# Mean squares by one block product instead of column sums and transposing spreads

## The chip, the cores and the metric

The kernel runs on one core of one Trainium2 chip. The metric is the device time of a launch in microseconds (us); of two kernels the one with the smaller time is better. A core has TensorE (PE in the profile, its weight loads PEld), VectorE (DVE), ScalarE (ACT), GpSimd (POOL) and SyncE (SP), and DMA queues that SP, ACT and POOL issue to.

## The reference

A trunk of two layers over x of 512 positions by 1024 channels, all in float32. Each layer has two sub-layers:

```python
h = rms_norm(x, norm1_g[l])
proj = h @ w_in[l]
za, xb, q, k, v, g = jnp.split(proj, splits, axis=-1)
ya = spatial_gating(jax.nn.gelu(za), a_vnorm_g[l], a_ws[l], a_bs[l])
yb = multiscale_pool(xb, b_w[l], b_scale[l])
yc = retention(q, k, v, g, c_norm_g[l])
x = x + jnp.concatenate([ya, yb, yc], axis=-1) @ w_out[l]
x = x + conv_ffn(rms_norm(x, norm2_g[l]), w_up[l], conv_w[l], conv_b[l], w_down[l])
```

`rms_norm` divides a position's 1024 channels by the root of their mean square plus EPS = 1e-6. `retention` ends with a norm per head: eight heads of 64 channels, each with its mean taken off and divided by the root of its mean square plus EPS, then a gain, then a product with silu(g). A last `rms_norm` follows the second layer.

## The kernel before

Channels lie on partitions and the 512 positions on the free dimension: x is eight tiles X[k] of 128 channels by 512 positions. Weights come as slots of 1024 columns through SP's queue; each is split into a rounded part `hi` (ScalarE) and the rest `lo` (VectorE), and a product in near-float32 precision is three fast matmuls (`mm3`, lines 310 to 312: hi by hi, hi by lo, lo by hi). A few products run in plain fp32; the profile shows each of those as two records.

`mixing` computes the first sub-layer as a list of short steps, `MIX`, in program order. Q, K, G, B and U are projections of one slot, A one of two; s and y are the scores and the output of one head; v centres the values; B and m are pooling and its map; a is the spatial gating; r and c are the head norm. The framework orders each engine's instructions when the kernel is built, by this order, by planned costs and by which buffers are free, so the steps may overlap. At the end `oproj` forms each output tile from eight operands `cat`, in the order in which `MIX` finishes them, the first six of tiles 0 and 1 ahead of the last two.

Head norm. After two heads (a pair p) `ymix` leaves their output in a tile `y_sb` and its square in `ysq`. Step r, `yvar`, sums the squares of each head for 128 positions at a time: the square is the stationary operand and a table of two columns, `selt`, the moving one, so that the sums lie with positions on partitions (eight columns a pair). `rsqrt` computes the reciprocal square root on these small tiles, with a term from the table `epst`, by ScalarE's Sqrt, VectorE's reciprocal and one refinement step. Step c, `ycat`, spreads the result back to channels: for each head and each 128 positions, one column, broadcast, is the stationary operand and the identity the moving one. Then it multiplies `y_sb` by gain and factor, by the gate, and splits the product for `oproj`.

Second norm. `feed` collects the squares of X in one tile `s`. `stats` (line 291) sums it over channels in the same way into four columns and calls `rsqrt`; `spread` (line 298) brings the factor back to all 128 partitions and ScalarE copies it to `bc`. In `ffn` the first two up projections run ahead of the factor: `stats` follows the first, `spread` the second. Their results are multiplied by `bc` (line 725).

Other tiles of 512 columns come from one pool, `U`, of `UBUFS` = 58 buffers; PSUM has eight banks of one tile each.

Of the kernel before, what the change touches and what calls it, by code (L numbers as in the profile page):

```python
# [10 lines left out]
F32 = mybir.dt.float32  # L11
F32R = mybir.dt.float32r
AF = mybir.ActivationFunctionType
ALU = mybir.AluOpType
AX = mybir.AxisListType

P = 128
D = 1024
T = 512
DEPTH = 2  # L20
KT = D // P
NT = T // P
AW = 256
CW = 512
HEADS = 8
DH = 64
# [4 lines left out]
EPS = 1e-6  # L31

C_N1, C_N2, C_VG, C_BS, C_CG, C_CW, C_CB = 0, 8, 16, 18, 20, 24, 24 + 3 * 2 * FT
# [4 lines left out]
GROUPS = (8, 8, 6)  # L38
SLOTS_PER_LAYER = 98
WBUFS = {"raw": 5, "hi": 5, "lo": 5}  # L40
UBUFS = 58
LOOK = 3
FIN = 3
WARM = 9
MIX = (
    "Q0 K0 v23 G0 v01 Q1 s0 K1 G1 s1 y0 Q2 s2 y1 K2 s3 B0 y2 Q3 s4 y3 K3 "
    "m0 r01 s5 y4 A s6 G2 y5 G3 s7 y6 y7 r2 c1 c0 B1 r3 a U1 c2 c3 m1 U0"
).split()
WIDE = {"A": 2}
SLOT = {}  # L50
# [139 lines left out]
def trunk(ctx: ExitStack, tc: tile.TileContext, xT, wflat, vec, ws_t, bias_t, bw, rope, dmask, vdec, geps, cnt, sel, out):  # L190
    nc = tc.nc
    cp = ctx.enter_context(tc.tile_pool(name="const", bufs=1))
# [10 lines left out]
    def PS(name):  # L203
        return psp.tile([P, T], F32, tag="ps", name=name)
# [15 lines left out]
    make_identity(nc, ident)  # L220
    ones = cp.tile([P, 1], F32, name="ones")
    nc.vector.memset(ones, 1.0)
    eps = cp.tile([P, 1], F32, name="eps")
    nc.vector.memset(eps, EPS)
    selt = cp.tile([P, 2], F32, name="selt")
# [5 lines left out]
    nc.gpsimd.dma_start(out=dmt, in_=dmask)  # L231
    dect = cp.tile([P, NT, HEADS], F32, name="dect")
    nc.gpsimd.dma_start(out=dect, in_=vdec)
    epst = cp.tile([P, 4, NT, 2], F32, name="epst")
    nc.gpsimd.dma_start(out=epst, in_=geps)

    zero = U("zero", F32R)
    nc.vector.memset(f(zero), 0.0)
# [1 line left out]
    for i in range(WARM):  # L240
        nc.tensor.matmul(busy, zero[:, :P], zero, start=True, stop=True)

    def rsqrt(src, n, scale, name, eps_t=None):
        m = sp.tile([P, n], F32, tag="rm", name=name + "m")
        r0 = sp.tile([P, n], F32, tag="r0", name=name + "a")
        if eps_t is None:
            nc.vector.tensor_scalar(
                out=m, in0=src, scalar1=-0.5 * scale, scalar2=-0.5 * EPS, op0=ALU.mult, op1=ALU.add
            )
            nc.scalar.activation(out=r0, in_=src, func=AF.Sqrt, scale=scale, bias=eps)  # L250
        else:
            nc.vector.scalar_tensor_tensor(
                out=m, in0=src, scalar=-0.5 * scale, in1=eps_t, op0=ALU.mult, op1=ALU.subtract
            )
            nc.scalar.activation(out=r0, in_=m, func=AF.Sqrt, scale=-2.0)
        nc.vector.reciprocal(r0, r0)
        nc.vector.tensor_tensor(out=m, in0=m, in1=r0, op=ALU.mult)
        nc.vector.tensor_tensor(out=m, in0=m, in1=r0, op=ALU.mult)
        r = sp.tile([P, n], F32, tag="rr", name=name + "r")
        nc.vector.scalar_tensor_tensor(out=r, in0=m, scalar=1.5, in1=r0, op0=ALU.add, op1=ALU.mult)  # L260
        return r

    class Norm:
        def __init__(self, name, col):
# [4 lines left out]
        def feed(self, k):  # L269
            n = f"{self.name}_{k}"  # L270
            g = vecs[:, self.col + k : self.col + k + 1]
            hi = U(n + "h", F32R)
            lo = U(n + "l", F32R)
            nc.scalar.activation(out=hi, in_=X[k], func=AF.Identity, scale=g)
            nc.vector.scalar_tensor_tensor(out=lo, in0=X[k], scalar=g, in1=f(hi), op0=ALU.mult, op1=ALU.subtract)
            self.h.append(hi)
            self.l.append(lo)
            sq = U(n + "q")
            nc.scalar.activation(out=sq, in_=X[k], func=AF.Square)
            if k == 0:  # L280
                self.s = sq
                warm = sp.tile([P, 1], F32, tag="warm", name=n + "w")
                nc.scalar.activation(out=warm, in_=sq[:, :1], func=AF.Sqrt)
            else:
                nc.vector.tensor_tensor(out=self.s, in0=self.s, in1=sq, op=ALU.add)

# [7 lines left out]
        def spread(self):  # L294
            n = self.name
            rb = PS(n + "rb")
            for b in range(NT):
                nc.tensor.matmul(
                    rb[:, b * P : (b + 1) * P],
                    self.tok[:, b : b + 1].to_broadcast([P, P]),  # L300
                    ident,
                    start=True,
                    stop=True,
                )
            self.bc = U(n + "bc")
            nc.scalar.copy(self.bc, rb)

    def mm3(ps, wt, k, xh, xl, first, last, more=False):
        hi, lo = wt
# [34 lines left out]
    def mixing(l, nm, nxt):  # L344
# [4 lines left out]
        def col(c):  # L349
            return vecs[:, vc + c : vc + c + 1]  # L350
# [97 lines left out]
        y_sb = {}  # L448
        yn = {}
# [48 lines left out]
        yr = {}  # L498

        def yvar(ps):  # L500
            n = 2 * NT
            vps = PS(f"yv{l}_{ps[0]}")
            for i, p in enumerate(ps):
                sq = ysq.pop(p)
                for b in range(NT):
                    o = i * n + 2 * b
                    nc.tensor.matmul(vps[:, o : o + 2], sq[:, b * P : (b + 1) * P], selt, start=True, stop=True)
            m = n * len(ps)
            et = epst[:, ps[0] : ps[-1] + 1].rearrange("p a b o -> p (a b o)")
            r = rsqrt(vps[:, :m], m, 1.0 / DH, f"yr{l}_{ps[0]}", et)  # L510
            for i, p in enumerate(ps):
                yr[p] = r[:, i * n : (i + 1) * n]

        def ycat(p):
            r = yr.pop(p)
            rb = PS(f"yb{l}_{p}")
            for b in range(NT):
                for o in range(2):
                    nc.tensor.matmul(
                        rb[o * DH : o * DH + DH, b * P : (b + 1) * P],  # L520
                        r[:, 2 * b + o : 2 * b + o + 1].to_broadcast([P, DH]),
                        ident,
                        start=True,
                        stop=True,
                    )
            y = y_sb.pop(p)
            nc.vector.scalar_tensor_tensor(out=y, in0=y, scalar=col(C_CG + p), in1=rb, op0=ALU.mult, op1=ALU.mult)
            g = yn.pop(p)
            nc.vector.tensor_tensor(out=g, in0=g, in1=y, op=ALU.mult)
            cat[4 + p] = split(g, f"c{l}_{4 + p}")  # L530

# [175 lines left out]
    def ffn(l, nm, nxt):  # L707
# [4 lines left out]
        def up(j, s):  # L712
            c2 = []
            for which in range(2):
                n = f"{l}_{j}_{which}"
                ps = proj("up" + n, s + which, hs, ls)
                if j == 0:
                    (nm.spread if which else nm.stats)()
                c2.append(ps)
            for which, ps in enumerate(c2):  # L720
                n = f"{l}_{j}_{which}"
                t = which * FT + j
                w = [vecs[:, vc + C_CW + i * 2 * FT + t : vc + C_CW + i * 2 * FT + t + 1] for i in range(3)]
                u = U("uu" + n)
                nc.vector.tensor_tensor(out=u, in0=ps, in1=nm.bc, op=ALU.mult)  # L725
                c = U("cc" + n)
                nc.scalar.activation(  # L727
                    out=c, in_=u, func=AF.Identity, scale=w[2], bias=vecs[:, vc + C_CB + t : vc + C_CB + t + 1]
                )
                for d in (1, 2):  # L730
                    nc.vector.scalar_tensor_tensor(  # L731
                        out=c[:, d:], in0=u[:, : T - d], scalar=w[2 - d], in1=c[:, d:], op0=ALU.mult, op1=ALU.add
                    )
                if which == 0:
                    nc.scalar.activation(out=c, in_=c, func=AF.Silu)  # L735
                c2[which] = c
            nc.vector.tensor_tensor(out=c2[0], in0=c2[0], in1=c2[1], op=ALU.mult)
            return c2[0]

        def down(g, s, acts):  # L740
# [13 lines left out]
            def done(m):  # L754
                if g < LAST:
                    return
                if nxt is not None:
                    ready.add(m)
                    while len(nxt.h) in ready:
                        nxt.feed(len(nxt.h))  # L760
                    return
                sq = U(f"fq{m}")
                nc.scalar.activation(out=sq, in_=X[m], func=AF.Square)
                if not total:
                    warm = sp.tile([P, 1], F32, tag="warm", name="warm_f")
                    nc.scalar.activation(out=warm, in_=sq[:, :1], func=AF.Sqrt)
                    total.append(sq)
                else:
                    nc.vector.tensor_tensor(out=total[0], in0=total[0], in1=sq, op=ALU.add)
                scaled(m)  # L770
# [217 lines left out]
def _tables():  # L988
# [11 lines left out]
    dmask = np.where((s <= t)[None], 1.0, late).astype(f).transpose(1, 0, 2)  # L1000
    pos = (np.arange(NT)[None, :] * P + np.arange(P)[:, None]).astype(np.float64)
    vdec = (np.exp(-lg[None, None, :] * pos[:, :, None]) * DH**-0.5).astype(f)
    grow = 0.5 * EPS * np.exp(-2.0 * lg[None, None, :] * pos[:, :, None])
    geps = grow.reshape(P, NT, 4, 2).transpose(0, 2, 1, 3).astype(f)
    cnt = np.zeros((P, 2, 17), f)
    for i in range(2):
        for p in range(P):
# [95 lines left out]
```

## Time and profile before

| what | us |
|---|---|
| median of 3 runs (1129.53 to 1131.45) | 1129.67 |
| the profiled execution, its time | 1129.15 |
| its span, first to last instruction | 1127.4 |
| TensorE busy | 1119.7 |
| VectorE busy | 887.7 |
| ScalarE busy | 571.6 |

The rows further down come from the profiled execution; their times count from the start of its span. A matmul's length in a timeline reaches to its modelled end and overlaps the next one, so the distance between starts is what it takes of the queue. In the chain of waits every piece has the time that it adds.

### The profile page before, as it was taken

How to read it: one execution, taken by the hardware profiler on the slowest of the kernel's cores; microseconds unless marked ns; L12 is line 12 of the kernel's file. 1: busy time of each engine (PE TensorE's matmuls, PEld its weight loads, DVE VectorE, ACT ScalarE, POOL GpSimd, SP SyncE). 2: the span in 40 equal slices, each digit the busy share in tenths (PEclk: the TensorE clock that was granted, in tenths of full speed). 3: DMA queues.
4: the chain of work that ended last, by engine and by line, in shares of the span. 5: the costliest groups of instructions: out<-in, count | busy, mean ns of one | idle time of the engine just before them, and what ended most of it. 6: DMA issues, size and time to landing. Idle time of an engine off the chain costs nothing.

```text
span 1127.4 us, 15279 instructions
## 1 busy us (share of the span) xinstructions
PE 1119.7 (99%) x5916; PEld 960.1 (85%) x5916; DVE 887.7 (79%) x1416; ACT 571.6 (51%) x819; POOL 27.5 (2%) x71
## 2 busy tenths in 40 slices
PE   9999999999999999999999999999999999999997
PEld 7888888888898889988988898888889988898887
DVE  6998676589976898679958877656898688986885
ACT  7677745444434443344637785544544344433452
POOL 2010000000000000000001000000000000000000
PEclk9999999999999999999999999999999999999999
DMA  9443223221253312521444322233211522143112
GB/s 329 147 114 93 76 75 94 94 94 57 71 164 104 99 51 92 166 89 47 132 130 131 94 76 62 88 94 94 94 56 63 181 94 76 38 168 120 45 43 75
DMA packets 34568, 112.92 MB, mean 100 GB/s; under 512 B 4368, under 2 KB 6336, under 8 KB 34496
## 3 DMA queue, kind: packets, MB, share of 16 engines
q1 hardware_dynamic: 31152, 103.82, 28.5%
q0 software_dynamic: 2480, 6.87, 2.2%
q10 hardware_dynamic: 864, 1.26, 0.3%
q8 instruction: 46, 0.75, 0.3%
q14 instruction: 26, 0.21, 0.1%
HBM read 105.64 MB, written 2.10 MB: 96 GB/s over the span
## 4 chain that ended last, share of the span: by engine, by line
PE 97%; DMA 2%; ACT 0%; DVE 0%; issue 0%; ACTq 0%
PE up L310 14%; PE up L312 14%; PE up L311 14%; PE o L310 3%; PE o L312 3%; PE o L311 3%; PE dn L310 2%; PE dn L311 2%; PE dn L312 2%; DMA wr<-in_wflat_dram 1%; PE k L311 1%; PE q L312 1%; PE q L311 1%; PE k L312 1%; PE q L310 1%; PE g L311 1%
## 5 line engine op out<-in xcount | busy, mean ns | idle before, releaser
L136 ACT CAST wh<-wr 128x1024 fp32r<-128x1024 f32 x161 | 167.6, 1042 | 225.3 <-PE up L311 75.8
L137 DVE TENSOR_TENSOR wl<-wr,wh 128x1024 fp32r<-128x1024 f32 x161 | 194.8, 1211 | 31.9 <-ACT wh L136 29.3
L731 DVE SCALAR_TENSOR_TENSOR cc<-uu,vecs,cc 128x511 f32<-128x511 f32 (+1 forms) x176 | 128.9, 745 | 1.9 <-ACT cc L727 0.6
L727 ACT ACTIVATE cc<-uu,vecs 128x512 f32<-128x512 f32 x88 | 70.8, 812 | 17.6 <-DVE uu L725 17.1
L735 ACT ACTIVATE cc<-cc 128x512 f32<-128x512 f32 x44 | 27.8, 632 | 79.9 <-DVE cc L731 79.9
L725 DVE TENSOR_TENSOR uu<-up,n_1bc 128x512 f32<-128x512 f32 x44 | 30.0, 688 | 31.7 <-PE up L312 31.5
L725 DVE TENSOR_TENSOR uu<-up,n_0bc 128x512 f32<-128x512 f32 x44 | 30.0, 687 | 31.1 <-PE up L312 31.1
L157 ACT CAST pt<-ps 128x1024 fp32r<-128x1024 f32 (+1 forms) x30 | 30.3, 1010 | 47.6 <-DVE ps L151 10.9
L158 DVE TENSOR_TENSOR pu<-ps,pt 128x1024 fp32r<-128x1024 f32 (+1 forms) x30 | 35.0, 1168 | 5.3 <-PE dp_4c L312 4.3
L679 DVE TENSOR_TENSOR x<-x,o 128x512 f32<-128x512 f32 x16 | 11.0, 687 | 32.5 <-PE o L312 32.5
L310 PE MATMUL up<-n_0h,wh 128*128 128x512 f32 x88 | 34.6, 394 | 0.0
L310 PE MATMUL up<-n_1h,wh 128*128 128x512 f32 x88 | 34.3, 390 | 0.0
L311 PE MATMUL up<-n_0l,wh 128*128 128x512 f32 x88 | 34.3, 390 | 0.0
L312 PE MATMUL up<-n_0h,wl 128*128 128x512 f32 x88 | 34.3, 389 | 0.0
L310 PE MATMUL up<-n_2h,wh 128*128 128x512 f32 x88 | 34.3, 389 | 0.0
L312 PE MATMUL up<-n_2h,wl 128*128 128x512 f32 x88 | 34.3, 389 | 0.0
L311 PE MATMUL up<-n_1l,wh 128*128 128x512 f32 x88 | 34.3, 389 | 0.0
L312 PE MATMUL up<-n_1h,wl 128*128 128x512 f32 x88 | 34.3, 389 | 0.0
L311 PE MATMUL up<-n_3l,wh 128*128 128x512 f32 x88 | 34.3, 389 | 0.0
L311 PE MATMUL up<-n_5l,wh 128*128 128x512 f32 x88 | 34.3, 389 | 0.0
L312 PE MATMUL up<-n_4h,wl 128*128 128x512 f32 x88 | 34.2, 389 | 0.0
L310 PE MATMUL up<-n_6h,wh 128*128 128x512 f32 x88 | 34.2, 389 | 0.0
(2395 smaller groups left out, 3540.0 us busy)
## 6 DMA issues: line engine op xcount, KB each, us to landing
wr<-in_wflat_dram SPq DMA_DIRECT2D x159, 512.0 KB, 3.5
pq<-in_wflat_dram SPq DMA_DIRECT2D x12, 512.0 KB, 3.4
pr<-in_wflat_dram SPq DMA_DIRECT2D x12, 512.0 KB, 3.5
wr<-in_wflat_dram SPq DMA_DIRECT2D x8, 256.0 KB, 7.7
x<-in_xT_dram SPq DMA_DIRECT2D x8, 256.0 KB, 7.4
pq<-in_wflat_dram SPq DMA_DIRECT2D x3, 384.0 KB, 3.1
pr<-in_wflat_dram SPq DMA_DIRECT2D x3, 384.0 KB, 3.2
qs_0h<-qs_0h POOLq DMA_DIRECT2D x8, 128.0 KB, 2.2
```

What stands on the lines that cost most here:

```text
L136: nc.scalar.copy(h, raw)
L137: nc.vector.tensor_tensor(out=o, in0=raw, in1=h.bitcast(F32), op=ALU.subtract)
L157: nc.scalar.copy(h, x)
L158: tt(out=lo, in0=x, in1=h.bitcast(F32), op=ALU.subtract)
L310: nc.tensor.matmul(ps, hi[:, k, :], xh, start=first, stop=False, skip_group_check=more)
L311: nc.tensor.matmul(ps, hi[:, k, :], xl, start=False, stop=False, skip_group_check=more)
L312: nc.tensor.matmul(ps, lo[:, k, :], xh, start=False, stop=last, skip_group_check=more)
L679: nc.vector.tensor_tensor(out=X[m], in0=X[m], in1=ps, op=ALU.add)
L725: nc.vector.tensor_tensor(out=u, in0=ps, in1=nm.bc, op=ALU.mult)
L727: nc.scalar.activation(out=c, in_=u, func=AF.Identity, scale=w[2], bias=vecs[:, vc + C_CB + t : vc + C_CB + t + 1])
L731: nc.vector.scalar_tensor_tensor(out=c[:, d:], in0=u[:, : T - d], scalar=w[2 - d], in1=c[:, d:], op0=ALU.mult, op1=ALU.add)
L735: nc.scalar.activation(out=c, in_=c, func=AF.Silu)
```

## The change

It has five parts. The sums of the squares of a pair's heads are formed by one fp32 product with a 128x128 block matrix `heads` (1/64 within each head's block), so that every channel row of the result holds its head's mean square at all 512 positions; a new function, `refine`, takes the reciprocal square root on that full tile, and `ycat` uses it as it is. The term that stood in `epst` is now a full tile for each pair, loaded from HBM in step r. The second layer norm uses one such product with `mean` (1/1024 everywhere), in `average`, in place of `stats` and `spread`. `rsqrt`, which the other norms keep, uses ScalarE's Abs_reciprocal_sqrt instead of Sqrt and VectorE's reciprocal. `MIX` has the steps r one by one and later, and another order of c, U and m; `UBUFS` falls to 57.

```diff
-UBUFS = 58
+UBUFS = 57
...
-    "m0 r01 s5 y4 A s6 G2 y5 G3 s7 y6 y7 r2 c1 c0 B1 r3 a U1 c2 c3 m1 U0"
+    "m0 s5 y4 A s6 G2 y5 G3 r0 s7 y6 r1 y7 r2 c0 B1 c1 a r3 U1 c2 U0 c3 m1"
...
+    mean = cp.tile([P, P], F32, name="mean")
+    nc.vector.memset(mean, 1.0 / D)
+    heads = cp.tile([P, P], F32, name="heads")
+    nc.vector.memset(heads, 0.0)
+    for i in range(2):
+        nc.vector.memset(heads[i * DH : (i + 1) * DH, i * DH : (i + 1) * DH], 1.0 / DH)
...
-    epst = cp.tile([P, 4, NT, 2], F32, name="epst")
-    nc.gpsimd.dma_start(out=epst, in_=geps)
...
-    def rsqrt(src, n, scale, name, eps_t=None):
+    def rsqrt(src, n, scale, name):
...
+        nc.scalar.activation(out=r0, in_=src, func=AF.Abs_reciprocal_sqrt, scale=scale, bias=eps)
...
-        nc.vector.reciprocal(r0, r0)
...
+    def refine(out, x, name):
+        r0, sq = U(name + "0"), U(name + "1")
+        nc.scalar.activation(out=r0, in_=x, func=AF.Abs_reciprocal_sqrt)
+        nc.scalar.activation(out=sq, in_=r0, func=AF.Square)
+        nc.vector.scalar_tensor_tensor(out=sq, in0=x, scalar=-0.5, in1=sq, op0=ALU.mult, op1=ALU.mult)
+        nc.vector.scalar_tensor_tensor(out=out, in0=sq, scalar=1.5, in1=r0, op0=ALU.add, op1=ALU.mult)
...
-                nc.scalar.activation(out=warm, in_=sq[:, :1], func=AF.Sqrt)
+                nc.scalar.activation(out=warm, in_=sq[:, :1], func=AF.Abs_reciprocal_sqrt)
...
+        def average(self):
+            rb = PS(self.name + "rb")
+            nc.tensor.matmul(rb, mean, self.s, start=True, stop=True)
+            self.bc = U(self.name + "bc")
+            nc.vector.tensor_scalar(out=self.bc, in0=rb, scalar1=EPS, scalar2=None, op0=ALU.add)
+            refine(self.bc, self.bc, self.name + "b")
...
         def yvar(ps):
...
+            for p in ps:
+                et = U(f"et{l}_{p}")
+                nc.gpsimd.dma_start(out=et, in_=geps[p])
+                vps = PS(f"yv{l}_{p}")
+                nc.tensor.matmul(vps, heads, ysq.pop(p), start=True, stop=True)
+                nc.vector.tensor_tensor(out=et, in0=vps, in1=et, op=ALU.add)
+                refine(et, et, f"er{l}_{p}")
+                yr[p] = et
...
         def ycat(p):
...
-            rb = PS(f"yb{l}_{p}")
-            for b in range(NT):
-                for o in range(2):
-                    nc.tensor.matmul(
-                        rb[o * DH : o * DH + DH, b * P : (b + 1) * P],
-                        r[:, 2 * b + o : 2 * b + o + 1].to_broadcast([P, DH]),
-                        ident,
-                        start=True,
-                        stop=True,
-                    )
...
+            y, r, g = y_sb.pop(p), yr.pop(p), yn.pop(p)
+            nc.vector.scalar_tensor_tensor(out=y, in0=y, scalar=col(C_CG + p), in1=r, op0=ALU.mult, op1=ALU.mult)
...
-                if j == 0:
-                    (nm.spread if which else nm.stats)()
+                if j == 0 and which == 0:
+                    nm.average()
```

## Rows read from the trace of the kernel before

**Rows 1.** The page's busy times of the engines, with share and instructions.

```profile
PE 1119.7 (99%) x5916; PEld 960.1 (85%) x5916; DVE 887.7 (79%) x1416; ACT 571.6 (51%) x819; POOL 27.5 (2%) x71
```

**Rows 2.** All waits of TensorE: us in total, times, longest.

```profile
PE busy L241 <- DVE zero L238: 1.5, 1, 1.5
PE fss L906 <- DVE fq L878: 1.0, 1, 1.0
```

**Rows 3.** Stretches ending mixing: length, busy PE, PEld, DVE, ACT, POOL, clock, DMA share.

```profile
102.00:133.00 31.00, 31.00 (x200) 28.02 (x200) 22.36 (x47) 25.80 (x46) 1.54 (x3) 1.00 0.28 80
133.00:165.80 32.80, 32.80 (x225) 27.07 (x225) 27.43 (x52) 15.78 (x25) 2.46 (x9) 1.00 0.24 77
...
686.80:719.60 32.80, 32.80 (x226) 27.03 (x225) 27.37 (x52) 15.71 (x24) 0.11 (x1) 1.00 0.18 58
```

**Rows 4.** TensorE in order of time, output projection: start, length, instruction.

```profile
169.70 0.39 PE L310 MATMUL o<-c_3h,wh 128*128 128x512 f32 x1
169.92 0.39 PE L311 MATMUL o<-c_3l,wh 128*128 128x512 f32 x1
170.15 0.39 PE L312 MATMUL o<-c_3h,wl 128*128 128x512 f32 x1
```

**Rows 5.** TensorE in order of time around the head sums, end of mixing.

```profile
144.75 0.95 PE L507 MATMUL yv<-selt,ysq 128*128 128x2 f32 x8
145.63 1.97 PE L598 MATMUL sg<-wst,va 128*64 128x128 f32 x32
...
152.87 0.39 PE L312 MATMUL u<-n_7h,wl 128*128 128x512 f32 x1
153.19 1.09 PE L519 MATMUL yb<-ident,yr_2r 128*64 128x128 f32 x16
...
155.09 1.12 PE L574 MATMUL bm<-pl,bwt 128*128 128x512 f32 x2
...
156.28 0.40 PE L311 MATMUL u<-n_0l,wh 128*128 128x512 f32 x1
```

**Rows 6.** Chain of waits, same stretch: start us, us added, engine and line.

```profile
102.00 0.86 PE bm L574 x2
...
135.76 0.58 PE yb L519 x6
...
137.07 1.67 PE yb L519 x26
138.74 0.43 PE xb L310
...
155.16 1.05 PE bm L574 x2
```

**Rows 7.** TensorE in order of time around the second layer norm.

```profile
210.50 0.95 PE L291 MATMUL n_0ss<-ones,n_0q 128*128 128x1 f32 x8
...
211.63 0.40 PE L311 MATMUL up<-n_0l,wh 128*128 128x512 f32 x1
...
216.89 1.05 PE L298 MATMUL n_0rb<-ident,n_0r 128*128 128x128 f32 x8
...
218.01 0.39 PE L311 MATMUL up<-n_0l,wh 128*128 128x512 f32 x1
```

**Rows 8.** Groups on VectorE, 133 to 165.8 us: count, busy us, mean ns.

```profile
L527 DVE SCALAR_TENSOR_TENSOR ysb<-ysb,vecs,yb 128x512 f32<-128x512 f32 x4 | 2.8, 729 | 1.6 <-PE yb L519 1.6
...
L622 DVE TENSOR_TENSOR us<-u,n_0bc 128x512 f32<-128x512 f32 x2 | 1.4, 692 | 1.3 <-PE u L312 1.3
...
L258 DVE TENSOR_TENSOR yr_2m<-yr_2m,yr_2a 128x8 f32<-128x8 f32 x1 | 0.2, 168 | 0.0
```

**Rows 9.** One group on ScalarE, whole span.

```profile
L495 ACT ACTIVATE ysq<-ysb 128x512 f32<-128x512 f32 x8 | 5.1, 634 | 1.5 <-DVE ysb L492 1.5
```

**Rows 10.** DMA issues: queue, count, KB each, median us to landing.

```profile
cos<-in_rope_dram POOLq DMA_DIRECT2D x2, 256.0 KB, 4.3
```

**Rows 11.** VectorE in order of time: the last operand of the output projection.

```profile
165.11 0.69 DVE L213 TENSOR_TENSOR c_0l<-us,c_0h 128x512 fp32r<-128x512 f32 x1 [0.69 <-ACT c_0h L212]
```

**Rows 12.** GpSimd in order of time; in brackets its idle time before.

```profile
528.36 0.54 POOL L360 DMA_DIRECT2D cos<-in_rope_dram  x1 [371.31 <-PE up L312]
```

More of the change, by code (lines that the diff above doesn't have):

```diff
@@ L241, in trunk @@
         nc.tensor.matmul(busy, zero[:, :P], zero, start=True, stop=True)
-    def rsqrt(src, n, scale, name, eps_t=None):
+    def rsqrt(src, n, scale, name):
         m = sp.tile([P, n], F32, tag="rm", name=name + "m")
         r0 = sp.tile([P, n], F32, tag="r0", name=name + "a")
-        if eps_t is None:
-            nc.vector.tensor_scalar(
-                out=m, in0=src, scalar1=-0.5 * scale, scalar2=-0.5 * EPS, op0=ALU.mult, op1=ALU.add
-            )
[L250 to L255, printed above, removed]
-        nc.vector.reciprocal(r0, r0)
+        nc.vector.tensor_scalar(
+            out=m, in0=src, scalar1=-0.5 * scale, scalar2=-0.5 * EPS, op0=ALU.mult, op1=ALU.add
+        )
+        nc.scalar.activation(out=r0, in_=src, func=AF.Abs_reciprocal_sqrt, scale=scale, bias=eps)
         nc.vector.tensor_tensor(out=m, in0=m, in1=r0, op=ALU.mult)
@@ L500, in yvar @@
         def yvar(ps):
[L501 to L504, printed above, removed]
-                for b in range(NT):
[L506 to L512, printed above, removed]
-        def ycat(p):
-            r = yr.pop(p)
-            rb = PS(f"yb{l}_{p}")
-            for b in range(NT):
-                for o in range(2):
-                    nc.tensor.matmul(
-                        rb[o * DH : o * DH + DH, b * P : (b + 1) * P],
-                        r[:, 2 * b + o : 2 * b + o + 1].to_broadcast([P, DH]),
-                        ident,
-                        start=True,
-                        stop=True,
[L525 to L528, printed above, removed]
+            for p in ps:
[6 more added lines that the diff above has]
+                yr[p] = et
+        def ycat(p):
+            y, r, g = y_sb.pop(p), yr.pop(p), yn.pop(p)
+            nc.vector.scalar_tensor_tensor(out=y, in0=y, scalar=col(C_CG + p), in1=r, op0=ALU.mult, op1=ALU.mult)
             nc.vector.tensor_tensor(out=g, in0=g, in1=y, op=ALU.mult)
@@ L765, in done @@
                     warm = sp.tile([P, 1], F32, tag="warm", name="warm_f")
-                    nc.scalar.activation(out=warm, in_=sq[:, :1], func=AF.Sqrt)
+                    nc.scalar.activation(out=warm, in_=sq[:, :1], func=AF.Abs_reciprocal_sqrt)
                     total.append(sq)
@@ L1002, in _tables @@
     vdec = (np.exp(-lg[None, None, :] * pos[:, :, None]) * DH**-0.5).astype(f)
-    grow = 0.5 * EPS * np.exp(-2.0 * lg[None, None, :] * pos[:, :, None])
-    geps = grow.reshape(P, NT, 4, 2).transpose(0, 2, 1, 3).astype(f)
+    grow = EPS * np.exp(-2.0 * lg[:, None] * np.arange(T)[None, :])
+    geps = np.repeat(grow, DH, axis=0).reshape(HEADS // 2, P, T).astype(f)
     cnt = np.zeros((P, 2, 17), f)
```

## The prediction

> **What bounds the kernel now.** I read the busy times first, because they say which engine can pay for a change at all. TensorE is busy 1119.7 of 1127.4 us, VectorE 79%, ScalarE 51% [rows 1]. A busy TensorE can still be one that waits between short bursts, so the waits of that engine come next: there are two, 1.5 us for the zero tile at the start and 1.0 us for the last sums at the end [rows 2]. In between its queue never stands still. So a matmul that goes saves its own time, one that comes costs its own time, and work of any other engine costs nothing as long as it stays ahead of TensorE's queue. The third view is the table of stretches. I cut it at the end of the mixing stage, where the edits fall; the second layer's stretch answers to the first's [rows 3]. From 133.0 to 165.8 us TensorE is busy throughout, VectorE for 27.43 of the 32.80 us, ScalarE for 15.78. VectorE has 5.4 us to spare, and that is the margin to watch.
>
> **The change part by part.** A 512-column fp32r matmul follows the one before at a regular pitch of 0.23 us [rows 4]. I cost a group of fp32 matmuls from its first start to the regular matmuls behind it, so that a late start after a change of format is counted with it.
>
> *Sums of the heads (yvar).* Each pair's four products with two columns go (eight records, since an fp32 product shows as two passes). One such group starts at 144.75, the next line's matmul at 145.63: 0.88 us [rows 5]. Four a layer: 3.52 us.
>
> *Spreading the head norms (ycat).* 32 transposing products a layer go. Those of the first two pairs take 0.58 + 1.67 us in the chain of waits, and the xb matmul behind them takes 0.43 in place of 0.23: 2.45 us [rows 6]. The other two start at 153.19, which is 0.32 instead of 0.23 behind the u matmul ahead of them, and the bm behind them starts at 155.09: 1.90 + 0.09 = 1.99 us [rows 5]. Together 4.44 us.
>
> *Second layer norm (stats and spread).* The ss group starts at 210.50, and the second up matmul behind it at 211.63; less the one regular pitch between, 0.90. The rb group runs the same way from 216.89 to 218.01: 0.89. Together 1.79 us [rows 7].
>
> A layer so sheds 3.52 + 4.44 + 1.79 = 9.75 us of TensorE's time.
>
> *The five new block products a layer* (four with heads, one with mean) are 128x128 fp32 on 512 columns, the same form as bm, which is in the trace. The bm ahead of fp32r work starts at 155.09 and the second u matmul behind it at 156.28: 1.19 - 0.23 = 0.96 us [rows 5]. In the chain of waits bm stands with 0.86 where other fp32 work follows, and with 1.05 where fp32r work does [rows 6]. I take 0.96, since the new ones mostly stand among fp32r work; 0.86 and 1.05 are the bounds. Five make 4.8 us.
>
> Net 4.95 us a layer, 9.9 us in two. Upper bound: 2 x (9.75 - 5 x 0.86) = 10.9. For the lower one I take a late start of 0.09 off each of the eight removed groups, 9.03, and 1.05 for the new: 2 x (9.03 - 5.25) = 7.6 us.
>
> *VectorE and ScalarE.* Each of the four refinements of a layer brings an addition out of PSUM (0.69 us) and two scalar-tensor-tensors (0.73) on VectorE [rows 8], and two ScalarE activations (0.63) [rows 9]: 2.15 and 1.26 us, so 8.6 and 5.0 us a layer, where ten small VectorE operations of 0.17 us stood in the same stretch [rows 8]. The mean product brings the same 2.15 and 1.26 us to the start of the feed-forward stage and takes away five small operations and a copy. Its factor is ready 0.96 + 2.15 + 1.26 = 4.4 us and some hand-overs after 210.50, ahead of the old one, whose rb product only started at 216.89 [rows 7]. I cost all of this at nothing, because TensorE's queue hides it. For ScalarE that is safe: 17 us idle in the stretch [rows 3]. For VectorE it is not, and the first rival is the price if the cover fails. The reciprocals that go from the other norms are on no path of TensorE's: nothing.
>
> *Loads.* The small table of epsilons goes, and a 256 KB row of it is fetched for each pair, eight in all, through GpSimd's queue, where others of this size land 4.3 us after issue [rows 10]; DMA is busy 18 to 28% there [rows 3]. Behind them in that queue stand only the clears for the second pooling and the next layer's constants. A late load holds back its addition and a PSUM bank. The last of them belongs to c3, whose squares were summed at 144.75 [rows 5], while the first operand of the late pair is used at 169.70 [rows 4]: 25 us, less the 2.4 us that TensorE gets shorter there (first rival). The steps between are the product, the refinement, ycat and the split, 0.96 + 2.15 + 1.26 + 0.73 + 0.69 + 0.63 + 0.69 = 7.1 us by the same rows. That leaves some 15 us, so I put nothing; a load later than that costs its excess.
>
> *The new memsets* on VectorE, four ahead of zero, lengthen the wait of 1.5 us at the start [rows 2]. What waits are warming matmuls whose result nobody reads, so nothing; doubling the wait, 1.5 us, is the other bound.
>
> *Later order.* The operands that come last are now those of c3 and m1 instead of m1 and U0. Before, the last lo part was started at 165.11 [rows 11], 4.6 us ahead of the use at 169.70 [rows 4]; the room is weighed in the first rival.
>
> The sum stands against the profiled execution, 1129.15 us: 1129.15 - 9.9 = 1119.25. The median of the runs is 1129.67, half a microsecond above it, so the runs should have 1119.3 to 1119.8; I say 1119.5.
>
> **The rivals.** A difference under 0.2% (2.3 us) is about what a measurement of this kernel can't tell from no change.
>
> *VectorE becomes the bound at the end of the mixing stage.* Its 27.4 us in the stretch become 27.4 + 8.6 - 1.7 = 34.3. TensorE took 36.7 us from 133.0 to the first late operand at 169.70; it loses two yv (1.76) and the yb (4.44) and gains four products (3.84), so 34.3. That is a tie with no gap left on VectorE. If its 5.4 us of gaps stay, TensorE stands for up to 5.4 us a layer, less what it can take ahead (the first six operands of a further output tile are 18 x 0.23 = 4.1 us). For this speaks the tie. Against it: VectorE has 8.6 us free from 102 to 133 us [rows 3], where the first refinements may run, and the queue's order fills such holes already (yb stands in two pieces, x6 and x26 [rows 6]). Half of the gaps give 2 x 2.7 us, 1125; all of them 1130. I give 17% to a part of it (1122 to 1127.4) and 7% to all, which is no change.
>
> *Buffers, the slower side.* The pool of 512-column tiles falls from 58 to 57, squares and head outputs are held longer, and each refinement takes three tiles more. That this pool is tight shows in the load of cos for layer two: issued at 528.36, after its queue had idled 371 us, and released by an up matmul [rows 12]. If the scores of the last heads wait for tiles, their products and with them c3 move back. It makes the kernel slower only where it costs over 9.9 + 2.3 = 12.2 us, 6.1 a layer; with 15 us of cover behind the last head that asks for 21 us of delay a layer, and gives 1132 or more. The same could come from the feed-forward stages, at 2 us for each of their six ends of a group. Against it: no wait of TensorE for a tile shows now. 10%.
>
> *The new products run at the pitch of the fp32r ones.* If each pass took 0.23 us [rows 4], a product would cost 0.46 and the saving would be 2 x (9.75 - 2.3) = 14.9: 1114.6 us. The bm rows, the same form, show 0.86 and more, so 2%. The Trainium skill (TensorE: Matmul & The Clock Gate, section "Back-to-back issue gap") puts a warm matmul at N/2.4 + 2.5 ns, an estimate of 216 ns for 512 columns. By that rule this rival would hold; the trace comes near it for fp32r (0.23 us) and shows about twice it for a pass in fp32.
>
> **How the numbers follow.** The forecast holds 64%: 7.6 to 10.9 us off, 1118.3 to 1122.1 with the half microsecond to the median. The range, 1118.0 to 1126.5, takes in the forecast's bounds and most of the partial rival; it leaves out the tie in full, the buffers and the fast products. Faster 0.64 + 0.17 + 0.02 = 0.83, same 0.07, slower 0.10.
>
> **What would show it.** In the changed profile: yv as eight products of two passes over 512 columns, none of the transposing yb, each new product within 0.86 to 1.05 us, TensorE's busy time near 1110 us and its waits still two. Wrong it would be if TensorE waits for a late operand (c_7 or c_3) in the output projection (VectorE), or for a score's hi or lo part in y (buffers), or if the new products have another price.

## The result: slower, by a term that the sum did not have

The changed kernel takes 1140.49 us (median of 4 runs, 1138.83 to 1140.72), the one before 1129.81 (1129.53 to 1131.45, 4 runs): ratio 1.0089 [1.0077, 1.0101]. Forecast were 1119.5 us and a faster kernel; it is 0.9% slower, a small difference, but clear of the noise. The profiled execution took 1140.46 us with a span of 1138.7.

The busy line of the page of the changed kernel, which answers to [rows 1]:

```profile
PE 1129.0 (99%) x5712; PEld 945.2 (83%) x5712; DVE 901.2 (79%) x1404; ACT 577.4 (51%) x827; POOL 31.4 (3%) x78
```

TensorE runs 204 matmuls fewer, which is what the edits remove and add, and is busy 9.3 us longer. Its waits after the change, against [rows 2] (us in total, times, longest):

```profile
PE busy L245 <- DVE zero L242: 1.8, 1, 1.8
PE y L490 <- ACT S_0h L212: 1.6, 2, 0.8
PE fss L901 <- DVE fq L873: 1.0, 1, 1.0
PE v L350 <- ACT n_0h L278: 0.4, 1, 0.4
```

One wait of weight is new, 0.8 us a layer for a score's hi part. With the others, the waits grew by 2.3 us. The rest of the loss therefore lies inside TensorE's busy time.

The timeline by landmarks tells where. The second layer norm of layer one starts at 210.50 before [rows 7] and at 210.75 after, so the mixing stage gave no net saving. From there to the first layer norm of layer two (579.37 and 585.10) it is 368.87 us before and 374.35 after. That stage is the feed-forward one, in which the change only makes the norm at its start cheaper. Yet it lost 5.5 us, and layer two's lost 6.2 from its norm to the final one (764.22 to 1110.07 before, 769.57 to 1121.57 after). So something made matmuls dearer that the diff does not contain. TensorE in order of time in that stage (start, length, instruction), on the same operands, first in the kernel before and then in the changed one:

```profile
298.28 0.39 PE L311 MATMUL dn<-G_1al,wh 128*128 128x512 f32 x1
...
299.87 0.39 PE L312 MATMUL dn<-G_3ah,wl 128*128 128x512 f32 x1
```

```profile
299.68 0.39 PE L322 MATMUL dn<-G_1al,wh 128*128 128x512 f32 x1
299.91 0.39 PE L323 MATMUL dn<-G_1ah,wl 128*128 128x512 f32 x1
...
301.07 0.40 PE L322 MATMUL dn<-G_3al,wh 128*128 128x512 f32 x1
301.31 0.39 PE L323 MATMUL dn<-G_3ah,wl 128*128 128x512 f32 x1
```

Before, the seven steps from 298.28 to 299.87 take 1.59 us, 0.227 each; after, those from 299.68 to 301.31 take 1.63 us, 0.233 each. Over all neighbouring 512-column matmuls of a trace whose starts are 205 to 260 ns apart (this leaves out waits and the two records of an fp32 product), the mean distance, called pitch from here on, is 227.04 ns before and 232.76 after. With some 3,760 such pairs the 5.72 ns make about 21.5 us. The lengths in the timeline, 0.39 and 0.40, are too coarse to show it. The mean lengths of groups do show it: one and the same group of untouched matmuls has 389 ns before (first line) and 395 after:

```profile
L312 PE MATMUL up<-n_1h,wl 128*128 128x512 f32 x88 | 34.3, 389 | 0.0
```

```profile
L323 PE MATMUL up<-n_1h,wl 128*128 128x512 f32 x88 | 34.8, 395 | 0.0
```

The new product, in order of time at the second layer norm of the changed kernel (answers to [rows 7]):

```profile
210.75 1.02 PE L314 MATMUL n_0rb<-n_0q,mean 128*128 128x512 f32 x2
211.21 0.80 PE L321 MATMUL up<-n_0h,wh 128*128 128x512 f32 x1
211.84 0.39 PE L322 MATMUL up<-n_0l,wh 128*128 128x512 f32 x1
```

Measured as the prediction measured it: 211.84 - 210.75 = 1.09, less one pitch of 0.23: 0.86 us. That is the lower of the two bounds, 0.10 below the value taken.

### The profile page after: what moved, and what is told of

Its sections match the earlier page's. It is cut to its first block, busy times and chain, and to the rows that moved or that the text cites. A ratio compares the mean times of both kernels' runs of the same rounds, so it can differ in the third digit from the quotient of the medians.

```text
span 1138.7 us, 14884 instructions
## 1 busy us (share of the span) xinstructions
PE 1129.0 (99%) x5712; PEld 945.2 (83%) x5712; DVE 901.2 (79%) x1404; ACT 577.4 (51%) x827; POOL 31.4 (3%) x78
## 4 chain that ended last, share of the span: by engine, by line
PE 98%; ACT 1%; DVE 0%; DMA 0%; issue 0%; SPq 0%; ACTq 0%
PE up L323 14%; PE up L322 14%; PE up L321 14%; PE o L322 3%; PE o L321 3%; PE o L323 3%; PE dn L321 3%; PE dn L323 3%; PE dn L322 3%; PE v L350 1%; PE v L351 1%; PE q L321 1%; PE g L322 1%; PE v L352 1%; PE k L323 1%; PE q L322 1%
## 5 line engine op out<-in xcount | busy, mean ns | idle before, releaser
L322 PE MATMUL up<-n_6l,wh 128*128 128x512 f32 x88 | 34.8, 395 | 0.0
L321 PE MATMUL up<-n_7h,wh 128*128 128x512 f32 x88 | 34.8, 395 | 0.0
L322 PE MATMUL up<-n_2l,wh 128*128 128x512 f32 x88 | 34.8, 395 | 0.0
L323 PE MATMUL up<-n_3h,wl 128*128 128x512 f32 x88 | 34.8, 395 | 0.0
L322 PE MATMUL up<-n_4l,wh 128*128 128x512 f32 x88 | 34.8, 395 | 0.0
L321 PE MATMUL up<-n_5h,wh 128*128 128x512 f32 x88 | 34.8, 395 | 0.0
L323 PE MATMUL up<-n_7h,wl 128*128 128x512 f32 x88 | 34.8, 395 | 0.0
L321 PE MATMUL up<-n_3h,wh 128*128 128x512 f32 x88 | 34.8, 395 | 0.0
L323 PE MATMUL up<-n_5h,wl 128*128 128x512 f32 x88 | 34.8, 395 | 0.0
```

Of the source, the lines that this page charges most:

```text
L321: nc.tensor.matmul(ps, hi[:, k, :], xh, start=first, stop=False, skip_group_check=more)
L322: nc.tensor.matmul(ps, hi[:, k, :], xl, start=False, stop=False, skip_group_check=more)
L323: nc.tensor.matmul(ps, lo[:, k, :], xh, start=False, stop=last, skip_group_check=more)
```

## The experiments

What could slow matmuls that were not edited? The change places two constants of 512 bytes a partition (mean, heads) ahead of the pool of 512-column tiles and takes epst, 128 bytes, away. This pool so starts 896 bytes later in SBUF: from byte 35552 to 36448. The tiles of the weights' hi parts start at 184800 before and at 183264 after, 1536 bytes lower, because one 512-column buffer (2048) and 384 bytes of small tiles went as well. Modulo 256, the 512-column tiles moved from 224 to 96 and the weights stayed at 224. My theory after the result was that these places set the pitch; the rivals were the number of buffers (57 for 58) and the waits of VectorE or ScalarE. The ratios below are to the kernel before, measured beside each kernel.

**The changed kernel at the old places.** `mean` and `heads` move behind the 512-column tiles (pool `gap1`), and idle bytes there, ahead of them and ahead of the weights (`gap2`) put every other pool back to its old start.

```diff
-    mean = cp.tile([P, P], F32, name="mean")
+    mean = gap1.tile([P, P], F32, name="mean")
...
-    heads = cp.tile([P, P], F32, name="heads")
+    heads = gap1.tile([P, P], F32, name="heads")
...
+    pad0 = cp.tile([P, 32], F32, name="pad0")
...
+    pad1 = gap1.tile([P, 256], F32, name="pad1")
...
+    pad2 = gap2.tile([P, 96], F32, name="pad2")
```

> The changed kernel in which every tile of the pools (512-column tiles, padded, small, raw, hi and lo weights) starts at the same byte offset in SBUF as in the kernel before; the two constant matrices lie where the 58th buffer lay. The whole reference is computed. Theory of places (the offsets of the tiles set the pitch of a matmul): the pitch of a 512-column matmul goes from 232 back to 227 ns and the time falls by some 20 us, to 1119 to 1121. Theory of the program (the order of instructions, the waits and the work of the other engines set it): the pitch stays at 232 ns and the time at 1139 to 1141. Theory of the buffers (57 instead of 58): as the program's, since 57 remain.

Measured: 1122.89 us, ratio 0.9943 [0.9926, 0.996], pitch 227.1 ns. The same instructions at other addresses are 17.6 us faster than the changed kernel. That is 2 us above the range of the theory of places; two waits, treated further down, account for it.

**The kernel before at the new places**, with both pools moved (57 buffers, 896 idle bytes ahead of the 512-column tiles, 1664 ahead of the weights).

```diff
-UBUFS = 58
+UBUFS = 57
...
+    pad0 = cp.tile([P, 224], F32, name="pad0")
...
+    pad2 = gap2.tile([P, 416], F32, name="pad2")
```

> The kernel before with 57 buffers and idle pads, so that the 512-column tiles start at the changed kernel's offsets and the weight tiles at the changed kernel's offsets modulo 2048. The whole reference is computed. Theory of places: pitch 232 ns and some 20 us more, 1149 to 1151. Theory of the program: pitch 227 ns, 1129 to 1132. Theory of the buffers: slower by waits of TensorE, with the pitch at 227.

Measured: 1150.93 us (2 runs), ratio 1.0185 [1.0165, 1.0206], pitch 232.6 ns. An unchanged computation loses 21.1 us.

**The kernel before with one pool moved**, first the 512-column tiles alone (by 896 bytes, with 57 buffers), then, in another kernel, the weights alone (by 512 bytes, with 58):

```diff
-UBUFS = 58
+UBUFS = 57
...
+    pad0 = cp.tile([P, 224], F32, name="pad0")
...
+    pad1 = gap1.tile([P, 288], F32, name="pad1")
```

```diff
+    pad2 = gap2.tile([P, 128], F32, name="pad2")
```

> The kernel before with 57 buffers; only the 512-column tiles are moved by 896 bytes, all other pools stay. The whole reference is computed. Theory of places: if the moving operands' offset counts, pitch 232 ns and about 1150; if the weights' offset counts, 227 ns and 1130. Theory of the program: 227 ns, 1130. Theory of the buffers: 1130 plus waits of TensorE.

> The kernel before with 58 buffers; only the raw, hi and lo weight tiles are moved by 512 bytes. The whole reference is computed. Theory of places: if the weights' offset counts, pitch 232 ns and about 1150; if the moving operands' counts, 227 ns and 1130. Theories of the program and of the buffers: 227 ns, 1130.

Measured: 1150.30 us (2 runs), 1.018 [1.016, 1.02], with a pitch of 232.6 ns, for the 512-column tiles; 1129.90, 1.0001 [0.9991, 1.0012], for the weights. The busy line and the waits of the first of them:

```profile
PE 1140.7 (99%) x5916; PEld 962.3 (84%) x5916; DVE 889.6 (77%) x1416; ACT 572.0 (50%) x819; POOL 27.6 (2%) x73
```

```profile
PE busy L247 <- DVE zero L244: 1.5, 1, 1.5
PE fss L912 <- DVE fq L884: 1.0, 1, 1.0
```

As many matmuls and the same two waits as in [rows 1, 2], and 21.0 us more busy time. This is how a slower pitch looks in a page: nothing new to wait for, and longer records. A move of the weights by 512 bytes costs nothing; why became plain only with the scan.

**A scan of offsets.** Ahead of the kernel run 96 series of 21 fp32r matmuls, 128x128 on 512 columns. In the first 64 the moving operand starts 0, 32, 64 ... bytes further on, while the stationary one stays; in the other 32 the stationary one moves too. Both tiles start at 224 modulo 256.

```diff
+    def probe(name, m, s, n=21):
+        ps = PS(name)
+        for i in range(n):
+            nc.tensor.matmul(ps, sta[:, s + i % 2 * 128 : s + i % 2 * 128 + P], mov[:, m : m + T], start=i == 0, stop=i == n - 1)
+    for m in range(0, 512, 8):
+        probe(f"pm{m}", m, 0)
+    for s in range(0, 256, 16):
+        for m in (0, 32):
+            probe(f"pq{s}x{m}", m, s)
```

> The kernel before with 55 buffers, and ahead of its work 96 series of 21 fp32r matmuls of 512 columns on zeros, with two stationary tiles in turn: 64 series with the moving operand at byte offsets 0 to 2016 from its tile's start (a step of 32), then 32 series with the stationary operand at 16 offsets, a step of 64, for two places of the moving one. Nothing is left out of the reference; only the pitch of the series is read, not the kernel's time. Theory of places: the pitch takes 227 ns at the offset that answers to the kernel before (256 bytes), 232 at the one that answers to the changed kernel (1152), and repeats with some power of two; the stationary operand's offset changes nothing. Rival, that the pitch comes from the accesses of other engines or from the stationary operand meeting the moving one: one pitch in the whole first scan, or a pitch that moves in the second.

The pitch, worked out from the start times in its trace (mean over the last 15 steps of a series, ns; the very first series, whose first steps are 427 ns apart, is left out):

```
moving operand +bytes       0      32     64     96     128    160    192    224
stationary +0            226.7  233.5  228.9  233.7  233.1  234.3  233.3  233.5
(within 0.1 the same in every further 256 bytes)

stationary +bytes         0      64     128    192
moving +0              226.7  233.2  232.4  228.9
moving +128            233.0  228.9  228.1  233.2
```

That the stationary operand's place would change nothing was wrong; the rival that the two operands' places meet was right. The other half of it, accesses of other engines, is out: from 100 to 470 us of this trace VectorE, ScalarE and GpSimd are busy 0.00 us, and the pitches differ by offset all the same. What the two tables agree on is the difference, moving less stationary, modulo 256: at 0 it is 226.7 and 228.1, at 64 it is 228.9 all three times, at all others 232 to 234. At one difference the place still counts a little (226.7 and 228.1; 232.4 and 233.1). For the products of weights with 512-column tiles, the kernel before has difference 0, the changed one 128. Moving the weights by 512 bytes left the difference at 0.

**Buffers.** The kernel before with 57 buffers and its places kept; the changed kernel with 58 at the old places (`mean` and `heads` in a pool `end` behind the weights, and idle bytes for the rest).

```diff
-UBUFS = 58
+UBUFS = 57
...
+    pad1 = gap1.tile([P, 512], F32, name="pad1")
```

```diff
-UBUFS = 57
+UBUFS = 58
...
-    mean = cp.tile([P, P], F32, name="mean")
+    mean = end.tile([P, P], F32, name="mean")
```

> The kernel before with 57 buffers, every pool at its old offset (the 58th buffer's place lies idle). The whole reference is computed. Theory of places: 1129.5 to 1130.5, pitch 227 ns. Theory that one buffer fewer costs: over 1132, with new waits of TensorE.

> The changed kernel at the old offsets with 58 buffers (the two constant matrices lie behind the weights). The whole reference is computed. With 57 buffers it took 1122.9, of which 3.0 us are four waits of TensorE in the output of the heads. If the 57 buffers cause those waits: they go, and 1119.5 to 1120.5 is left. If the order of VectorE's and ScalarE's queues causes them: they stay, and 1122 to 1123.5.

Measured: 1129.95 us, ratio 1.0 [0.999, 1.0011], and 1122.95, ratio 0.9939 [0.9923, 0.9956], beside 1122.89 with 57. The buffer is worth nothing in either kernel.

**The difference alone.** The changed kernel exactly as it is, with 128 idle bytes ahead of the weight tiles, so that both kinds of tile start at 96 modulo 256.

```diff
+    gap2 = ctx.enter_context(tc.tile_pool(name="gap2", bufs=1))
...
+    pad2 = gap2.tile([P, 32], F32, name="pad2")
```

> The changed kernel as it is, with 57 buffers and its own offsets of the 512-column tiles, and one idle pad of 128 bytes in front of the weight tiles, so that these start at the same offset modulo 256 bytes as the 512-column tiles (96 for both; in the kernel before both have 224). The whole reference is computed. Theory that the difference of the two offsets sets the pitch: near 227 ns, at most the 228.1 that the scan showed with both moved by 128, and 1122.5 to 1128. If the place of the 512-column tiles counts by itself: 232 ns and 1139 to 1141.

Measured: 1122.86 us, ratio 0.9941 [0.9923, 0.9959]. Its TensorE in the same stretch, and then all its waits:

```profile
299.21 0.39 PE L327 MATMUL dn<-G_7ah,wl 128*128 128x512 f32 x1
299.44 0.39 PE L325 MATMUL dn<-G_7bh,wh 128*128 128x512 f32 x1
...
300.80 0.39 PE L325 MATMUL dn<-G_7bh,wh 128*128 128x512 f32 x1
```

```profile
PE busy L249 <- DVE zero L246: 1.8, 1, 1.8
PE y L494 <- ACT S_0h L213: 1.6, 2, 0.8
PE y L499 <- DVE S_2l L214: 1.3, 2, 0.7
PE fss L905 <- DVE fq L877: 1.0, 1, 1.0
```

Seven steps take 1.59 us, 0.227 each. So 128 bytes that nobody uses give back 17.6 us, while the 512-column tiles, their number, `mean` and `heads` stay where the changed kernel has them. With the pitch mended a second new wait shows, which the changed kernel does not have: 0.65 us a layer for a score's lo part.

**Another difference: 64 bytes.** The kernel before with its 512-column tiles 64 bytes further on.

```diff
-UBUFS = 58
+UBUFS = 57
...
+    pad0 = cp.tile([P, 16], F32, name="pad0")
...
+    pad1 = gap1.tile([P, 496], F32, name="pad1")
```

> The kernel before with 57 buffers and the 512-column tiles moved by 64 bytes, all other pools at their old offsets. The whole reference is computed. The scan gave 226.7 ns where moving and stationary operand start at the same offset modulo 256 bytes, 228.9 at 64 bytes more and 233 at 128 bytes. Theory that this difference sets the pitch: 228.5 to 229.5 ns, and a third of the 20.5 us that the 896 bytes cost (they are 128 modulo 256), 1136 to 1138. If any misplacement costs the same: 1149 to 1151. If only some larger step counts: 1130.

Measured: 1132.77 us, ratio 1.0024 [1.0009, 1.004]. The pitch of 512 columns came out near the scan, 229.2 ns, but the loss was 3.1 us and not 7. The 256-column matmuls got quicker, from 119.8 to 117.1 ns: some 1,570 pairs of them make -4.2 us beside +8.3, and the profiled spans differ by 4.3. A scan at one width does not give the time of a kernel with two.

**The two waits that are left.** The chains that make them can be read. The first in the changed kernel as it is, ScalarE and then TensorE in order of time; the bracket is idle time and what ended it:

```profile
134.09 1.28 ACT L262 ACT_TABLE_LOAD   x1
135.95 0.63 ACT L262 ACTIVATE er<-et 128x512 f32<-128x512 f32 x1 [0.58 <-DVE et L517]
136.61 0.63 ACT L263 ACTIVATE er<-er 128x512 f32<-128x512 f32 x1
137.15 0.57 ACT L212 CAST S_0h<-sc 128x512 fp32r<-128x512 f32 x1
```

```profile
137.77 0.49 PE L490 MATMUL y<-S_0h,vv 128*128 128x512 f32 x1 [0.80 <-ACT S_0h L212]
```

The first refinement's table load, its wait for VectorE and its two activations stand in ScalarE's queue ahead of the hi part of a score, for which TensorE stands. In the kernel before this hi part was started at 133.48, and the table load came behind it, at 134.45. The other wait, in the changed kernel at the old places with 58 buffers, VectorE and then TensorE:

```profile
105.08 0.68 DVE L215 TENSOR_TENSOR S_2l<-sc,S_2h 128x512 fp32r<-128x512 f32 x1
```

```profile
105.82 0.45 PE L502 MATMUL y<-S_2l,vv 128*64 128x256 f32 x2 [0.70 <-DVE S_2l L215]
```

In the kernel before, VectorE and then TensorE:

```profile
105.04 0.68 DVE L213 TENSOR_TENSOR S_2l<-sc,S_2h 128x512 fp32r<-128x512 f32 x1
```

```profile
105.52 0.95 PE L507 MATMUL yv<-selt,ysq 128*128 128x2 f32 x8
...
106.65 0.40 PE L484 MATMUL y<-S_2l,vv 128*64 128x256 f32 x2
```

There the lo part was started as early as here, and its use came only at 106.65, because a head sum (yv) stood ahead of it. Without that group, and with less work before it, TensorE arrives first. If that reading holds, both waits go when other work stands ahead of the two uses. The next kernel changes, from the changed one at the old places with 58 buffers, nothing but `MIX`: A (the spatial gating's first projection) goes ahead of y4, and r0 and r1 go back by two places.

```diff
-    "m0 s5 y4 A s6 G2 y5 G3 r0 s7 y6 r1 y7 r2 c0 B1 c1 a r3 U1 c2 U0 c3 m1"
+    "m0 s5 A y4 s6 G2 y5 G3 s7 y6 r0 y7 r1 r2 c0 B1 c1 a r3 U1 c2 U0 c3 m1"
```

> The changed kernel at the old offsets with 58 buffers, and two steps of MIX in other places: A ahead of y4, r0 behind y6 and r1 behind y7. The whole reference is computed. If the four waits of TensorE (0.8 us each for the first score's hi part behind the refinement in ScalarE's queue, 0.7 us each for a lo part that VectorE starts at the same place as before while TensorE comes 0.7 us earlier) are what was missing: they go, and the time falls by 3.0 us from 1122.9 to 1119.5 to 1120.5. If the 3 us are lost in another way, or the waits only move: 1122 to 1123.5.

Measured: 1118.99 us (1118.63 to 1119.13), ratio 0.9905 [0.989, 0.992], the fastest of all and 10.7 us under the kernel before. All its waits:

```profile
PE busy L252 <- DVE zero L249: 1.8, 1, 1.8
PE fss L908 <- DVE fq L880: 1.0, 1, 1.0
PE v L357 <- ACT n_2h L285: 0.3, 1, 0.3
```

Both waits are gone. The time fell by 4.0 us, though, and they were 3.0; the rest was not taken apart.

**The old order.** The changed kernel (old places, 58 buffers) with the old `MIX`.

```diff
-    "m0 s5 y4 A s6 G2 y5 G3 r0 s7 y6 r1 y7 r2 c0 B1 c1 a r3 U1 c2 U0 c3 m1"
+    "m0 r01 s5 y4 A s6 G2 y5 G3 s7 y6 y7 r2 c1 c0 B1 r3 a U1 c2 c3 m1 U0"
```

> The changed kernel at the old offsets with 58 buffers and the MIX of the kernel before, so that the sums of heads are not moved. The whole reference is computed. If the later place of the sums is needed because VectorE is nearly full around 82 to 106 us: TensorE waits there by more than now, 2 to 4 us a layer, 1124 to 1128. If the place does not matter: 1120 to 1123.

Measured: 1142.42 us, ratio 1.0105 [1.0088, 1.0121], far outside what either theory gave. Its largest waits, and two stretches, each with its length, the busy time of PE, PEld, DVE, ACT and POOL, and TensorE's granted clock, the DMA share and GB/s:

```profile
PE sc L477 <- DVE S_0l L215: 5.4, 2, 2.7
PE bm L576 <- DVE pl L571: 4.7, 2, 2.3
PE yv L523 <- ACT ysq L513: 2.4, 2, 1.2
```

```profile
123.00:127.20 4.20, 1.16 (x7) 0.71 (x6) 4.18 (x9) 4.12 (x7) 0.00 (x0) 1.00 0.32 76
127.30:130.60 3.30, 3.30 (x9) 2.53 (x9) 2.72 (x5) 3.16 (x12) 0.15 (x1) 0.50 0.14 52
```

The refinements of pairs 0 and 1 then fall among the scores, and a later one stands in VectorE's queue ahead of the pooling (pl): waits of 12.5 us in these three groups. Behind the longest wait, in which TensorE works 1.16 of 4.2 us, the granted clock is 0.50 (1.2 GHz) in place of 1.00 (2.4 GHz) from 127.3 to 130.6 us, and 512-column matmuls start 0.43 us apart; layer two has two more such stretches, from 687.1 and from 721.2. All waits together grew by 11.5 us; the three stretches cost some 4 us, an estimate from seven steps of 0.43 instead of 0.23 us in each. The new order is worth 19.5 us to the changed kernel; as it moves steps of c, U and m too, how much of that is the later place of the sums is not shown.

**The second layer norm alone**: `mean` product as changed, and Abs_reciprocal_sqrt in `rsqrt`; head norms otherwise as before, everything else at its old place.

```diff
+    mean = end.tile([P, P], F32, name="mean")
...
-                if j == 0:
-                    (nm.spread if which else nm.stats)()
+                if j == 0 and which == 0:
+                    nm.average()
```

> Only the second layer norm by the mean product (and the new reciprocal square root in the small tiles); the head norms and MIX as in the kernel before, old offsets, 58 buffers. The whole reference is computed. By the sum of records, 1.79 us go and 0.96 come in each layer: 1.7 us off, 1128.0 to 1128.5, with no new wait. If the mean product's refinement delays the first up projections: over 1129.8.

Measured: 1127.47 us (1127.09 to 1130.52), ratio 0.9983 [0.9974, 0.9992], without a new wait of weight. It came out half a microsecond below the expected range. By the rows, with the measured 0.86, it should give 2 x (1.79 - 0.86) = 1.9 us; it gave 2.2.

## Why the prediction was wrong

**The step that failed** is the first sentence of the change part by part: "A 512-column fp32r matmul follows the one before at a regular pitch of 0.23 us". I read that pitch in one place [rows 4] and carried it over as a constant, so every matmul that the change keeps was costed at nothing. The change moved the pool of their operands by 896 bytes, 128 modulo 256, against the weights, and the pitch went from 227.04 to 232.76 ns: about 3,760 x 5.72 ns = 21.5 us, less 1.7 us for 256-column matmuls (119.8 to 118.7 ns). No rival named it. That it is the cause is shown both ways: in the kernel before the move alone costs 20.5 us, and in the changed one 128 idle bytes return 17.6. With these bytes the changed kernel takes 1122.86 us, faster than before and inside the stated range; what still parts it from 1119.5 are the two waits.

**The sum of the edits was right.** The groups named went, and the five products came at the price of the same form. Mis-sized was "I take 0.96": in the kernel with the two steps moved, eight of the ten products take 0.86 and only the two behind the gating's fp32 group 0.96, like the bm behind yb from which the price was taken. The saving is so 2 x (9.75 - 4 x 0.86 - 0.96) = 10.7 us, near the upper bound. That kernel shows 10.7, with TensorE busy 1108.7 us, where the prediction looked for 1110; that it agrees to the tenth is luck, since its waits are 0.6 us longer than before.

**The first rival was right in kind and wrong in place.** It looked for a late operand of the output projection; none came. After the change VectorE (the third busy time of the line below) works 29.30 us of the stretch of [rows 3], not 34.3: the refinements spread over more of the stage.

```profile
133.00:165.80 32.80, 32.00 (x161) 24.38 (x160) 29.30 (x48) 16.81 (x25) 3.55 (x11) 1.00 0.30 100
```

What came late were parts of scores, further ahead: a hi part, 0.8 us a layer, and with the pitch mended a lo part, 0.65. One waited for ScalarE, costed as "safe" by its idle total in the stretch; but a queue with 17 us idle can still be full ahead of one use. The prediction would have read "a score's hi or lo part in y" as a sign of the buffers; the two runs that change their number, and no place of the 512-column or weight tiles, rule that out.

**The buffers**, the only rival with a slower kernel, had the right sign by luck: they have nothing to do with it.

**Costed at nothing, rightly:** the loads, which land 2.9 us after issue here, with VectorE never idle ahead of the addition that uses them; the later norms' reciprocals; the products of the second norm ahead of their use. The wait for the zero tile grew by 0.3 us, within the bound given; what it is worth by itself wasn't tried. The later order was costed only as a risk at its end; the run with the old order shows that the change needs it.

**The account of the changed kernel**, profiled span against span: -10.7 (edits), +21.5 and -1.7 (pitch of 512 and of 256 columns), +2.3 (waits) give +11.4; the spans differ by 11.3. With the 128 idle bytes the same account is -10.7 and +3.2 of waits, -7.5, and the spans differ by -7.0.

**Open:** why the chip minds the difference of offsets; steps finer than 32 bytes, which weren't tried; and why the pitch at a difference of 128 takes two values, 232.4 and 233.3 ns: the changed kernel has the higher one from about 740 us on, the kernel before with the 512-column tiles moved from about 450 to 550 and again from about 1020.

## What to carry to other kernels

In a kernel whose TensorE never stands, a change that adds or drops a buffer also moves every tile behind it: before costing the edit, compare the start addresses of moving and stationary tiles modulo 256, and afterwards the start-to-start distance, or the mean length, of untouched matmuls in a stage that the change leaves alone. If it has moved, mend the layout first and judge the change after. A group of matmuls that goes can have been the cover of an operand behind it, and idle time summed over a stretch does not say that the queue is free ahead of one use.

## What the runs showed of the hardware

- The pitch of 512-column fp32r matmuls depends on the difference of the two operands' byte offsets modulo 256 (moving less stationary): 226.7 to 228.1 ns at 0, 228.9 at 64, 232 to 234 at the other multiples of 32 that were tried. On the kernel before, the move to 128 costs 1.8%.
- 256-column matmuls go otherwise: 119.8 ns at 0 and 117.1 at 64, but at 128 they take 118.7 in the changed kernel and 119.7 in the kernel before with its tiles moved, so for them this difference alone does not give the pitch.
- The mean length of a 512-column record moves with the pitch, from 389 to 395 ns; the two digits of a timeline hide it.
- An fp32 product of 128x128 on 512 columns takes 0.86 us, and 0.96 where another fp32 group stands ahead of it.
- With the old order TensorE worked 1.16 us of the 4.2 us up to 127.2; the granted clock then stood at 0.50 (1.2 GHz) up to 130.6 us, and was 1.00 (2.4 GHz) before and behind.
